# Delta rule inversion: the four steps with 64 wide f32 matmuls, tile by tile, become 128 wide matmuls of two tiles each

## The chip, the cores and the metric

The kernel runs on one core of one Trainium2 chip. The metric is the device time of one execution in microseconds (us), lower is better. A core has a matmul engine (TensorE, PE in the profile, with its weight loads as PEld), a vector engine (DVE), a scalar engine (ACT), GpSimd (POOL) and SyncE (SP, which issues most DMAs). Each engine works through its own queue in order; engines wait for each other by semaphores. Matmuls read their operands from the on-chip memory SBUF and write into PSUM banks, from which ACT and DVE copy results back.

## What is computed

A two-layer decoder trunk over 1024 positions and 1024 channels. The first layer mixes tokens by a gated DeltaNet, the second by a diagonal state-space layer; both run beside a cross-attention into 256 memory tokens, and both are followed by an MLP. The part that matters here is the DeltaNet's delta rule, per head and per chunk:

```
a_strict = jnp.where(strict, jnp.einsum('bhnid,bhnjd->bhnij', kb, k) * decay, 0.0)
sol = lax.linalg.triangular_solve(eye + a_strict, rhs, left_side=True, lower=True, unit_diagonal=True)
u_blk, w_blk = sol[..., :dv], sol[..., dv:]
def step(state, inp):
    v_new = ui - jnp.einsum('bhcd,bhde->bhce', wi, state)
    attn = jnp.einsum('bhid,bhjd->bhij', qi, ki) * deci
    o = (qi * exp(gci)) @ state + attn @ v_new
    state = state * jnp.exp(g_last) + k_dec^T @ v_new
```

There are 8 heads of width 128. The reference takes chunks of 64 positions; the kernel takes tiles of 128 positions, 8 tiles a head, and needs the inverse of one unit triangular 128 x 128 matrix (identity plus strictly triangular part) per head and tile.

## The kernel before

**The work and its stages.** Large products are made with three float32r matmuls each (`mm3`, L362 to L367: high x high, low x high, high x low parts of the operands), 128 x 512 a matmul. Small square products, the inversion among them, are single f32 matmuls. The stages are: projections of the first two heads; attention into the memory; the delta rule (`run`, the loop over heads): while the recurrence of head h runs (`gdn_recur`), the projections of head h + 1, the keys of head h + 3 and the inversion of head h + 1 are woven in as filling (`gdn_fill`); then the output projection, the MLP, and the second layer.

**The inversion.** The 128 x 128 triangular matrix is inverted from small blocks upward. `gdn_inverse` (L1079) inverts the diagonal 32 x 32 blocks of two heads at once on DVE, ACT and POOL and writes them to DRAM (`t32`, once as they are and once transposed), and `gdn_keys_out` (L1037) writes the negated strict part there (`ntf`). `gdn_invert_tiles` (L1169) does the rest, one head at a time in two halves of four tiles. Per half it loads `nm` (parts of `ntf`, three DMAs) and the block diagonals `T32` and `V32` (`block_diag`, L1161, two and four DMAs into the two buffers `bds`, which are cleared once at the start and used again for every half), and makes five steps:

1. `nm` times the first 32 x 32 blocks: four 64 wide matmuls (L1187); the result goes into `zi`, a buffer that begins as the identity, by an ACT copy (L1188) and a DVE copy (L1189).
2. `V32` times `zi`: four 64 wide matmuls (L1195), copied by ACT into the lower half of `o` (L1196).
3. `zi` times `V32`, 128 wide: four matmuls (L1202), copied by ACT into the result `TT` (L1203). It gives both 64 x 64 diagonal blocks of the inverse.
4. `nm`'s off-diagonal 64 x 64 block times `o`: four 64 wide matmuls over 64 rows (L1207), copied by DVE into the upper half of `o` (L1208).
5. `o` times `TT`: four 64 wide matmuls over 64 rows (L1212), copied by ACT into the off-diagonal block of `TT` (L1213).

All matmuls of the inversion are issued by the small helper `mm`, so that the profile has them under its line, L1176, and tells them apart by operands: `iv<-bd,nm`, `iv<-zi,bd`, `iv<-bd,zi`, `iv<-iv,nm`, `iv<-iv,iv`. All five results of a half go through one PSUM bank (tag `pi`, one buffer), so that a step's matmuls wait until the copies of the step before have read it. The buffers `nm`, `o`, `bds` and `zi` are of tag `h4`, which has six.

**What sets the order.** `settle` (L58 on) takes the whole traced program and writes out an order for every engine. It gives each instruction a price (`price`, L276), each PE instruction a due time from its place in the program, every other one a due time counted back from what needs it, and then issues whatever is ready and most pressing, engine by engine; a PE instruction may be taken up to 40 us ahead of its place. Prices of f32 matmuls go by the wider of the two operands, 0.01 us + 1.66 ns a column. A copy out of PSUM is made to wait for a copy by another engine that reads the same bank.

Of the kernel before, what the change touches and what calls it, by code (L numbers as in the profile page):

```python
# [10 lines left out]
F32 = mybir.dt.float32  # L11
# [5 lines left out]
P = 128  # L17
# [13 lines left out]
class Trunk:  # L31
# [810 lines left out]
    def gdn_consts(self):  # L842
        nc = self.nc
        scr = self.tile("scr", [P, 9 * P], F32, "scr")[:, :P + 8 + 13 * 64 + 96]
        self.small = [scr[:, P + 8 + n * 64:P + 8 + (n + 1) * 64] for n in range(13)]
        early = self.tile("h1", [P, 3 * P], F32, "early")
        U = early[:, 0:P]
        nc.gpsimd.memset(U, 1.0)
        nc.gpsimd.affine_select(U, U, [[1, P]], ALU.is_ge, 0.0, base=0, channel_multiplier=-1)
        self.U = U  # L850
        ones = early[:, P:2 * P]
        nc.gpsimd.memset(ones, 1.0)
        self.ones = ones
        mn = scr[:, 0:P]
        nc.gpsimd.memset(mn, 0.0)
        nc.gpsimd.affine_select(mn, mn, [[1, P]], ALU.is_ge, -1e30, base=0, channel_multiplier=-1)
        self.maskneg = mn
        self.early = [early[:, 2 * P + 64 * n:2 * P + 64 * (n + 1)].rearrange("p (t h) -> p t h", t=8) for n in range(2)]
        self.bds = [self.tile("h4", [P, 4, P], F32, "bd") for _ in range(2)]
        for o in self.bds:  # L860
            nc.gpsimd.memset(o, 0.0)
        self.zi = self.tile("h4", [P, 4, P], F32, "zi")
        nc.scalar.copy(self.zi, self.ident.unsqueeze(1).to_broadcast([P, 4, P]))
        cw = scr[:, P + 8 + 13 * 64:].rearrange("p (m j) -> p m j", j=4)
        nc.scalar.dma_start(cw, self.a["cw"])
        self.cw = cw
        ng = self.const("ng", [P, 1])
        nc.scalar.dma_start(ng, self.a["ng"])
        nc.gpsimd.tensor_scalar(ng, ng, 0.5, None, op0=ALU.mult)
        self.ng = ng  # L870
        self.kdd = self.dp.tile([8, 2, P, 4, P], F32, tag="kdd", name="kdd")
        self.ded = self.dp.tile([8, 2, P, 4, P], F32, tag="ded", name="ded")
        self.ntf = self.dp.tile([8, 2, P, 4, P], F32, tag="ntf", name="ntf")
        self.ntd = self.dp.tile([8, 8, 4, 32, 32], F32, tag="ntd", name="ntd")
        self.t32 = self.dp.tile([2, 8, 8, 4, 32, 32], F32, tag="t32", name="t32")
# [285 lines left out]
    def block_diag(self, h, hf, w):  # L1161

        o = self.bds[w]
        for b in (0, 2) if w == 0 else range(4):
            q = slice(32 * b, 32 * b + 32)
            self.nc.sync.dma_start(o[q, :, q], self.t32[w, h, 4 * hf:4 * hf + 4, b].rearrange("t i c -> i t c"))
        return o

    def gdn_invert_tiles(self, h):  # L1169


        nc = self.nc
        first = lambda x: x.rearrange("p (b k c) -> p b k c", b=2, k=2)[:, :, 0, :]
        zi = self.zi
        bank = lambda: self.psum("pi", "iv", (P, 4, P))
        mm = lambda *a: nc.tensor.matmul(*a, start=True, stop=True)  # L1176
        out = self.TT[h] = []
        for hf in range(2):
            nm = self.tile("h4", [P, 4, P], F32, "nm")
            for b in range(2):  # L1180
                nc.sync.dma_start(nm[:, :, 32 * b:32 * b + 32], self.ntf[h, hf, :, :, 64 * b + 32:64 * b + 64])
            nc.sync.dma_start(nm[0:64, :, 64:128], self.ntf[h, hf, 0:64, :, 64:128])
            T32, V32 = self.block_diag(h, hf, 0), self.block_diag(h, hf, 1)

            ps = bank()
            for t in range(4):
                mm(ps[0:64, t, 0:64], nm[:, t, 0:64], first(T32[:, t, :]))  # L1187
            nc.scalar.copy(zi[32:64, :, 0:32], ps[0:32, :, 0:32])  # L1188
            nc.vector.tensor_copy(zi[96:128, :, 64:96], ps[32:64, :, 32:64])  # L1189
            yield 0.5  # L1190

            o = self.tile("h4", [P, 4, 64], F32, "iv")
            ps = bank()
            for t in range(4):
                mm(ps[0:64, t, 0:64], V32[:, t, 0:64], zi[:, t, 0:64])  # L1195
            nc.scalar.copy(o[0:64], ps[0:64, :, 0:64])  # L1196
            yield 0.5

            TT = self.tile("h3", [P, 4, P], F32, "iv")
            ps = bank()  # L1200
            for t in range(4):
                mm(ps[:, t, :], zi[:, t, :], V32[:, t, :])  # L1202
            nc.scalar.copy(TT, ps)  # L1203
            yield 0.8
            ps = bank()
            for t in range(4):
                mm(ps[0:64, t, 0:64], nm[0:64, t, 64:128], o[0:64, t, :])  # L1207
            nc.vector.tensor_copy(o[64:128], ps[0:64, :, 0:64])  # L1208
            yield 0.5
            ps = bank()  # L1210
            for t in range(4):
                mm(ps[0:64, t, 0:64], o[64:128, t, :], TT[64:128, t, 64:128])  # L1212
            nc.scalar.copy(TT[0:64, :, 64:128], ps[0:64, :, 0:64])  # L1213
            out.append(TT)
            yield 0.5

# [1159 lines left out]
```

## Time and profile before

| what | value |
|---|---|
| median of 3 runs | 2592.98 us (2591.11 to 2593.45) |
| the profiled execution | 2591.98 us |
| its span, first to last instruction | 2590.3 us |
| mean granted TensorE clock | 0.995 |
| instructions | 36995 |
| bytes moved by DMA | 425.04 MB |
| PE matmuls at one place, L1176 | 640 records, from 182.4 to 667.2 us |

The profile is of one execution. Its rows give for a group of instructions the line, engine, operation, tiles as out<-in, form, count, then the busy time and the mean of one in ns, and behind the second bar the idle time of the engine just before them, with what ended it. The form of a matmul is first the part of the PE array that it uses, rows * columns, and then the size of what it reads or writes ("128*64 128x64"). A timeline row begins with start and length in us. One f32 matmul stands as two records of PE and two of PEld; a float32r matmul as one. A record's length is longer than the step from one matmul to the next, since they are pipelined.

### The profile page before, as it was taken

How to read it: one execution, taken by the hardware profiler on the slowest of the kernel's cores; microseconds unless marked ns; L12 is line 12 of the kernel's file. 1: busy time of each engine (PE TensorE's matmuls, PEld its weight loads, DVE VectorE, ACT ScalarE, POOL GpSimd, SP SyncE). 2: the span in 40 equal slices, each digit the busy share in tenths (PEclk: the TensorE clock that was granted, in tenths of full speed). 3: DMA queues.
4: the chain of work that ended last, by engine and by line, in shares of the span. 5: the costliest groups of instructions: out<-in, count | busy, mean ns of one | idle time of the engine just before them, and what ended most of it. 6: DMA issues, size and time to landing. Idle time of an engine off the chain costs nothing.

```text
span 2590.3 us, 36995 instructions
## 1 busy us (share of the span) xinstructions
PE 2527.0 (98%) x12525; PEld 2077.9 (80%) x12525; DVE 1968.6 (76%) x3659; ACT 1336.0 (52%) x2969; POOL 327.1 (13%) x445
## 2 busy tenths in 40 slices
PE   8999999999999999999999999989999999999998
PEld 6888788887787778878788888878877888888887
DVE  7675857566789988879988965663888766578779
ACT  6665665665446556454444245562456455454441
POOL 1111111010002123121220112212002000000000
PEclk9999999999999999999999999999999999999999
DMA  5443545455523766477354377764335444574422
GB/s 195 123 134 103 142 128 137 141 172 159 180 82 122 233 207 207 164 259 271 119 171 131 138 243 227 206 210 143 114 106 194 170 156 146 197 268 128 146 87 101
DMA packets 284638, 425.04 MB, mean 164 GB/s; under 512 B 114416, under 2 KB 131008, under 8 KB 284448
## 3 DMA queue, kind: packets, MB, share of 16 engines
q1 hardware_dynamic: 263632, 369.42, 43.5%
q0 software_dynamic: 18048, 48.75, 6.3%
q10 hardware_dynamic: 2768, 4.51, 0.5%
q8 instruction: 98, 1.61, 0.3%
q14 instruction: 92, 0.75, 0.1%
HBM read 286.79 MB, written 135.76 MB: 163 GB/s over the span
## 4 chain that ended last, share of the span: by engine, by line
PE 56%; DVE 5%; issue 2%; DMA 2%; ACT 1%; POOL 1%; SPq 0%; DVEq 0%; POOLq 0%; ACTq 0%
PE q L366 6%; PE q L365 6%; PE q L367 6%; PE pB L365 3%; PE pB L367 3%; PE pB L366 3%; PE pC L367 2%; PE pC L365 2%; PE pC L366 2%; PE pA L367 2%; PE pA L365 2%; PE pA L366 2%; PE wu L366 1%; PE tm L365 1%; PE wu L367 1%
## 5 line engine op out<-in xcount | busy, mean ns | idle before, releaser
L366 PE MATMUL q<-wkl,hkh 128*128 128x512 f32 x784 | 306.5, 391 | 0.9 <-DVE wkl L800 0.9
L365 PE MATMUL q<-wkh,hkh 128*128 128x512 f32 x784 | 306.6, 391 | 0.0
L367 PE MATMUL q<-wkh,hkl 128*128 128x512 f32 x784 | 304.7, 389 | 0.0
L799 ACT CAST wkh<-wr 128x512 fp32r<-128x512 f32 x168 | 104.9, 624 | 239.3 <-PE q L366 194.6
L365 PEld LDWEIGHTS q<-wkh,hkh 128*128 128x128 f32 x784 | 147.1, 188 | 33.5 <-issue 1.9
L366 PEld LDWEIGHTS q<-wkl,hkh 128*128 128x128 f32 x784 | 147.2, 188 | 31.4 <-DVE wkl L800 1.5
L367 PEld LDWEIGHTS q<-wkh,hkl 128*128 128x128 f32 x784 | 147.2, 188 | 30.6 <-issue 0.2
L365 PE MATMUL wi<-xTh,wih 128*128 128x512 f32 x384 | 160.4, 418 | 10.2 <-ACT wih L890 7.2
L800 DVE TENSOR_TENSOR wkl<-wr,wkh 128x512 fp32r<-128x512 f32 x168 | 115.6, 688 | 63.8 <-issue 50.5
L367 PE MATMUL wi<-xTh,wil 128*128 128x512 f32 x384 | 153.6, 400 | 0.5 <-DVE wil L345 0.5
L366 PE MATMUL wi<-xTl,wih 128*128 128x512 f32 x384 | 152.6, 397 | 0.0
L481 POOL TENSOR_TENSOR mv<-mv,mhalf 128x1 f32<-128x1 f32 x32 | 24.6, 767 | 879.0 <-DVE mv L480 879.0
L800 DVE TENSOR_TENSOR hkl<-hr,hkh 128x512 fp32r<-128x512 f32 x196 | 133.9, 683 | 1.9 <-ACT hkh L799 1.9
L799 ACT CAST hkh<-hr 128x512 fp32r<-128x512 f32 x196 | 120.8, 616 | 0.0
L365 PE MATMUL o<-ow,ok 128*128 128x512 f32 x256 | 102.3, 399 | 1.1 <-ACT ok L1608 0.6
L366 PE MATMUL o<-ow,ok 128*128 128x512 f32 x256 | 100.2, 392 | 0.2
L367 PE MATMUL o<-ow,ok 128*128 128x512 f32 x256 | 100.3, 392 | 0.1
L365 PEld LDWEIGHTS wi<-xTh,wih 128*128 128x128 f32 x384 | 72.9, 190 | 23.6 <-ACT wih L890 7.2
L367 PEld LDWEIGHTS wi<-xTh,wil 128*128 128x128 f32 x384 | 72.7, 189 | 15.6 <-DVE wil L345 1.0
L366 PEld LDWEIGHTS wi<-xTl,wih 128*128 128x128 f32 x384 | 73.1, 190 | 11.6
L793 DVE TENSOR_TENSOR y<-q,y 128x512 f32<-128x512 f32 x112 | 72.0, 680 | 0.0
L1608 ACT CAST ok<-os 128x512 fp32r<-128x512 f32 x56 | 34.9, 624 | 54.4 <-PE o L367 41.5
(586 smaller groups left out, 7423.7 us busy)
## 6 DMA issues: line engine op xcount, KB each, us to landing
hr<-hd SPq DMA_DIRECT2D x212, 256.0 KB, 2.6
wr<-in_w_dram SPq DMA_DIRECT2D x56, 512.0 KB, 4.5
w1r<-in_w_dram SPq DMA_DIRECT2D x48, 512.0 KB, 3.8
hd<-u SPq DMA_DIRECT2D x92, 256.0 KB, 2.0
hd<-hid SPq DMA_DIRECT2D x60, 256.0 KB, 3.5
hd<-p SPq DMA_DIRECT2D x60, 256.0 KB, 3.4
w1r<-in_w_dram SPq DMA_DIRECT2D x48, 256.0 KB, 4.7
wir<-in_w_in_dram SPq DMA_DIRECT2D x23, 512.0 KB, 4.0
```

Source lines behind the costliest of these rows:

```text
L365: mm(ps, a[0], b[0], start=start, stop=False, skip_group_check=onto)
L366: mm(ps, a[0], b[1], start=False, stop=False, skip_group_check=onto)
L367: mm(ps, a[1], b[0], start=False, stop=stop, skip_group_check=onto)
L481: nc.gpsimd.tensor_tensor(mv[:, 3:4], mv[:, 2:3], self.mhalf[:, 0:1], op=ALU.pow)
L793: V.tensor_tensor(o, bank[t], o, op=ALU.add)
L799: nc.scalar.copy(hi, s)
L800: nc.vector.tensor_tensor(lo, s, f32(hi), op=ALU.subtract)
L1608: nc.scalar.copy(hi, s)
```

## The change

Tiles are taken in pairs. With `left` of two tiles side by side as the stationary operand (2 x 64 columns) and `right` of the same two tiles as the moving one (2 x 64 columns), one matmul gives a 128 x 128 result, of which the two 64 x 64 corners on the diagonal are the two tiles' products; the other two corners aren't used. So each of steps 1, 2, 4 and 5 has two 128 wide matmuls instead of four 64 wide ones. Step 3 keeps its four.

To make the operands lie side by side, `nm` and `V32` get the layout 2 x 4 tiles x 64 columns. Steps 4 and 5 now go over all 128 rows: `nm[:, 1]` is loaded for all 128 partitions, and the upper half of `o` is cleared by a POOL memset before step 4 so that the added rows give nothing; in step 5 the added rows meet the block of `TT` that is still zero. A pair's two products lie on different partitions of the bank, and so each copy out of it becomes two: even tiles by ACT, odd tiles by DVE in steps 2, 4 and 5, and two by each in step 1.

```diff
-        self.bds = [self.tile("h4", [P, 4, P], F32, "bd") for _ in range(2)]
+        self.bds = [self.tile("h4", shape, F32, "bd") for shape in ([P, 4, P], [P, 2, 4, 64])]
...
-            self.nc.sync.dma_start(o[q, :, q], self.t32[w, h, 4 * hf:4 * hf + 4, b].rearrange("t i c -> i t c"))
+            to = o[q, :, q] if w == 0 else o[q, b // 2, :, 32 * (b % 2):32 * (b % 2) + 32]
+            self.nc.sync.dma_start(to, self.t32[w, h, 4 * hf:4 * hf + 4, b].rearrange("t i c -> i t c"))
...
+        def pairs(left, right):
+            ps = bank()
+            for t in (0, 2):
+                mm(ps[:, t // 2, :], left[:, t:t + 2].rearrange("p t c -> p (t c)"), right[:, t:t + 2])
+            return [ps[64 * x:64 * x + 64, 0:2, 64 * x:64 * x + 64] for x in range(2)]
...
-            nm = self.tile("h4", [P, 4, P], F32, "nm")
+            nm = self.tile("h4", [P, 2, 4, 64], F32, "nm")
             for b in range(2):
-                nc.sync.dma_start(nm[:, :, 32 * b:32 * b + 32], self.ntf[h, hf, :, :, 64 * b + 32:64 * b + 64])
-            nc.sync.dma_start(nm[0:64, :, 64:128], self.ntf[h, hf, 0:64, :, 64:128])
+                nc.sync.dma_start(nm[:, 0, :, 32 * b:32 * b + 32], self.ntf[h, hf, :, :, 64 * b + 32:64 * b + 64])
+            nc.sync.dma_start(nm[:, 1], self.ntf[h, hf, :, :, 64:128])
...
-            ps = bank()
-            for t in range(4):
-                mm(ps[0:64, t, 0:64], nm[:, t, 0:64], first(T32[:, t, :]))
-            nc.scalar.copy(zi[32:64, :, 0:32], ps[0:32, :, 0:32])
-            nc.vector.tensor_copy(zi[96:128, :, 64:96], ps[32:64, :, 32:64])
+            for x, q in enumerate(pairs(nm[:, 0], first(T32))):
+                nc.scalar.copy(zi[32:64, x::2, 0:32], q[0:32, :, 0:32])
+                V.tensor_copy(zi[96:128, x::2, 64:96], q[32:64, :, 32:64])
...
-            ps = bank()
-            for t in range(4):
-                mm(ps[0:64, t, 0:64], V32[:, t, 0:64], zi[:, t, 0:64])
-            nc.scalar.copy(o[0:64], ps[0:64, :, 0:64])
+            nc.gpsimd.memset(o[64:128], 0.0)
+            for x, q in enumerate(pairs(V32[:, 0], zi[:, :, 0:64])):
+                (nc.scalar.copy, V.tensor_copy)[x](o[0:64, x::2], q)
...
-                mm(ps[:, t, :], zi[:, t, :], V32[:, t, :])
+                mm(ps[:, t, :], zi[:, t, :], V32[:, :, t, :])
...
-            ps = bank()
-            for t in range(4):
-                mm(ps[0:64, t, 0:64], nm[0:64, t, 64:128], o[0:64, t, :])
-            nc.vector.tensor_copy(o[64:128], ps[0:64, :, 0:64])
+            for x, q in enumerate(pairs(nm[:, 1], o)):
+                (nc.scalar.copy, V.tensor_copy)[x](o[64:128, x::2], q)
...
-            ps = bank()
-            for t in range(4):
-                mm(ps[0:64, t, 0:64], o[64:128, t, :], TT[64:128, t, 64:128])
-            nc.scalar.copy(TT[0:64, :, 64:128], ps[0:64, :, 0:64])
+            for x, q in enumerate(pairs(o, TT[:, :, 64:128])):
+                (nc.scalar.copy, V.tensor_copy)[x](TT[0:64, x::2, 64:128], q)
```

In the changed file the matmuls' line is L1178, the copies are L1195, L1196 (step 1), L1202 (2), L1209 (3), L1212 (4) and L1215 (5), and the memset is L1200.

More of the change, by code (lines that the diff above doesn't have):

```diff
@@ L1172, in gdn_invert_tiles @@
         nc = self.nc
-        first = lambda x: x.rearrange("p (b k c) -> p b k c", b=2, k=2)[:, :, 0, :]
+        V = nc.vector
+        first = lambda x: x.rearrange("p t (b k c) -> p t b k c", b=2, k=2)[:, :, :, 0, :]
         zi = self.zi
```

## The prediction

> **What bounds the kernel now.** I read the page's busy table first, then the stage in which the inversion runs (180 to 668 us) as one window, then what the matmul engine (PE) waited for in it.
>
> ```profile
> PE 2527.0 (98%) x12525; PEld 2077.9 (80%) x12525; DVE 1968.6 (76%) x3659; ACT 1336.0 (52%) x2969; POOL 327.1 (13%) x445
> ```
> ```profile
> 180.00:668.00 488.00, 479.53 (x2888) 396.05 (x2887) 319.43 (x618) 292.51 (x953) 64.44 (x81) 1.00 0.51 150
> 668.00:2590.30 1922.30, 1879.12 (x8765) 1543.44 (x8763) 1518.59 (x2747) 924.95 (x1694) 237.59 (x317) 1.00 0.51 170
> ```
> ```profile
> PE wi L365 <- ACT qT L1008: 2.8, 2, 1.4
> ...
> PE iv L1176 <- DVE zi L1189: 0.5, 1, 0.5
> ```
>
> The first row is the stage of the inversion, the second the rest; the columns are length, then busy time of PE, its weight loads, DVE, ACT and POOL, then granted clock and DMA share. In the stage PE is busy 479.5 of 488.0 us at clock 1.00; DVE 319, ACT 293, POOL 64. The waits say the same: the longest kind of PE wait is 2.8 us in all, and for the inversion's own copies it waited once, 0.5 us. So here PE's queue sets the time, and what a matmul occupies of it is worth its full length. "Busy" doesn't say how much of that is streaming; for that I measure what a visit of the inversion costs between ordinary matmuls.
>
> **What a narrow visit costs.** I call the matmuls of one step that stand together a visit. It costs the time from the end of the instruction before it to the end of the one behind it, less that one's normal step. Each f32 matmul shows as two records, so x8 is a step of four.
>
> ```profile
> 184.08 0.40 PE L366 MATMUL wi<-xTl,wih 128*128 128x512 f32 x1
> 184.31 0.40 PE L367 MATMUL wi<-xTh,wil 128*128 128x512 f32 x1
> 184.64 0.68 PE L1176 MATMUL iv<-zi,bd 128*64 128x64 f32 x8
> 185.25 0.50 PE L365 MATMUL wi<-xTh,wih 128*128 128x512 f32 x1
> ```
>
> The normal step is 184.71 - 184.48 = 0.23. The visit: L367 ends at 184.71, the next L365 at 185.75; 1.04 - 0.23 = **0.81 us** for four 64 wide matmuls. Where the planner broke a step into one and three, the single one shows alone:
>
> ```profile
> 198.31 0.39 PE L365 MATMUL wz<-xTh,wzh 128*128 128x512 f32 x1
> 198.63 0.33 PE L1176 MATMUL iv<-zi,bd 128*64 128x64 f32 x2
> 198.89 0.50 PE L366 MATMUL wz<-xTl,wzh 128*128 128x512 f32 x1
> ```
>
> From 198.70 to 199.39, 0.69 - 0.23 = 0.46 us for one matmul. Three more cost 0.81 - 0.46 = 0.35, or 0.117 each. So a narrow visit has a **fixed part** of 0.46 - 0.117 = 0.343 us, nearly half of it. Now 128 wide visits, first the inversion's own third step, then four transposes (a record each):
>
> ```profile
> 187.20 0.40 PE L367 MATMUL wi<-xTh,wil 128*128 128x512 f32 x1
> 187.44 1.05 PE L1176 MATMUL iv<-bd,zi 128*128 128x128 f32 x8
> 188.25 0.47 PE L365 MATMUL wi<-xTh,wih 128*128 128x512 f32 x1
> ```
> ```profile
> 652.04 0.40 PE L367 MATMUL wz<-xTh,wzl 128*128 128x512 f32 x1
> 652.27 0.60 PE L1249 MATMUL vt<-ident,vT 128*128 128x128 f32 x4
> 652.63 0.48 PE L365 MATMUL wi<-xTh,wih 128*128 128x512 f32 x1
> ```
>
> The first: 188.72 - 187.60 - 0.23 = 0.89 us for eight records. The second: 653.11 - 652.44 - 0.23 = 0.44 for four. Twice the records cost twice the time: a 128 wide visit has no fixed part, and a 128 wide f32 matmul costs 0.89 / 4 = 0.2225 us. The weight loads' idle time tells the two kinds apart as well (the column behind the bar's second number):
>
> ```profile
> L1176 PEld LDWEIGHTS iv<-bd,zi 128*128 128x128 f32 x128 | 16.5, 191 | 1.3 <-DVE oT L1387 0.3
> ...
> L1176 PEld LDWEIGHTS iv<-zi,bd 128*64 128x64 f32 x128 | 8.9, 137 | 5.3 <-issue 2.2 <-DVE zi L1189 1.6 <-DVE gb L1235 0.4
> L1176 PEld LDWEIGHTS iv<-bd,nm 128*64 128x64 f32 x128 | 8.6, 137 | 5.1 <-issue 2.9 <-DMA bd<-t 0.7 <-ACT iv L1213 0.4
> L1176 PEld LDWEIGHTS iv<-iv,nm 64*64 64x64 f32 x128 | 8.6, 134 | 3.9 <-DVE oT L1387 1.1 <-ACT e L1351 0.7 <-ACT iv L1203 0.4
> L1176 PEld LDWEIGHTS iv<-iv,iv 64*64 64x64 f32 x128 | 8.6, 134 | 4.3 <-issue 2.9 <-DVE S L1360 0.4 <-DVE scr L1229 0.4
> ```
>
> The four narrow groups idle 18.6 us before their loads, the wide one 1.3, with as many records and in the same chain. Only the shape of the array that the matmul asks for differs (128*64 and 64*64 against 128*128). [...]
>
> **The change, part by part.** *Matmuls.* There are 8 heads x 2 halves x 4 narrow steps = 64 steps. In the built order of before they make 68 visits (60 whole, four broken in two): 256 x 0.117 + 68 x 0.343 = 30.0 + 23.3 = 53.3 us. After, all are 128 columns wide, two in a step: 128 x 0.2225 = 28.5. **Saved: 24.8 us**, nearly all of it the fixed part; streaming itself gains 1.5.
>
> *Order.* The planner orders the whole program anew, so other work could move. In the built order of the changed program PE's other matmuls stand as before up to the first inversion and again behind the last one; the same holds for ACT, DVE, POOL and SP. Only the delta rule's stretch is reshuffled. Behind it I count nothing: that stretch starts earlier and takes what it took.
>
> *Copies.*
>
> ```profile
> L1203 ACT COPY iv<-iv 128x512 f32<-128x512 f32 x16 | 9.5, 592 | 12.0 <-PE iv L1176 12.0
> ...
> L1208 DVE COPY iv<-iv 64x256 f32<-64x256 f32 x16 | 6.7, 418 | 12.4 <-PE iv L1176 11.9
> ...
> L1196 ACT COPY iv<-iv 64x256 f32<-64x256 f32 x16 | 5.9, 366 | 15.5 <-PE iv L1176 15.3
> L1213 ACT COPY iv<-iv 64x256 f32<-64x256 f32 x16 | 5.8, 366 | 14.7 <-PE iv L1176 14.4
> L1189 DVE COPY zi<-iv 32x128 f32<-32x128 f32 x16 | 4.6, 287 | 7.0 <-ACT zi L1188 6.8
> L1188 ACT COPY zi<-iv 32x128 f32<-32x128 f32 x16 | 4.1, 255 | 7.0 <-PE iv L1176 6.8
> ```
>
> A step's result now lies in two corners of the bank, so each copy becomes two, split over ACT and DVE. Per half of a head: the copies of 64x256 become ACT 64x128 and DVE 64x128 (128 elements a lane, as L1188 and L1189: 0.255 and 0.287); the first step's two become four of 64 elements a lane, estimated from the slopes between 128 and 256 elements at 0.20 on ACT and 0.22 on DVE. ACT goes from 1.58 to 1.76 us, DVE from 0.71 to 1.30: 2.9 and 9.5 us over 16 halves, beside 195 and 169 us in which they stand idle here. As work that is hidden. As a chain it is longer: L1189 waits for L1188 because both read one bank, so pairs run ACT, then DVE, and the first step ACT, DVE, ACT, DVE. First step 0.54 to 0.84, the next 0.37 to 0.54, the fourth 0.42 to 0.54, the fifth 0.37 to 0.54: 0.76 us a half without the hand-overs, at most **12.2 us** if PE had nothing to do meanwhile, zero if the work that the planner puts between steps covers it. In the new order most steps have 0.9 us or more of other matmuls between them, which covers 0.54 and a hand-over. Two places in head 6 don't: one matmul (0.22) between second and third step, two (0.46) between third and fourth, where the 0.59 copy of L1203 must pass. [...]
>
> *POOL's memset and the wait that it adds.* Sixteen memsets of 64x256; the nearest row is POOL's memset of the 128x512 tiles:
>
> ```profile
> L861 POOL MEMSET bd<- 128x512 f32 x2 | 1.0, 517 | 0.0
> ```
>
> Half the elements, about 0.26 us, 4 us in all on an engine idle 424 here. Each waits until step four of an earlier half has freed its buffer, and holds POOL's queue until then. The tightest place stands ahead of the next pair's "To" memsets:
>
> ```profile
> 252.57 0.99 POOL L1117 MEMSET To<- 128x512 f32 x2
> ```
> ```profile
> 264.48 0.68 PE L1176 MATMUL iv<-iv,nm 64*64 64x64 f32 x8
> ```
> ```profile
> 273.79 0.39 ACT L1123 COPY To<-X 64x64 f32<-64x64 f32 x2
> ```
>
> They would slip from 252.6 to about 265.4 + 0.3 + 1.0 = 266.7; ACT needs them at 273.8, so 7 us remain: zero. Without that cover a late memset would delay the pair's inversion by its lateness.
>
> *DMA.* As many issues as before; one load of each half has 128 partitions instead of 64. It is read in step four only, behind three steps: zero. If it came late, step four would wait for it alone.
>
> **Sum.** 24.8 - 1.5 = 23.3 us. The profiled execution took 2591.98 us (span 2590.3), 1.0 under the median of 2592.98; the difference carries over: 2592.98 - 23.3 = **2569.7 us**.
>
> **Rivals.** *The copies take over*: the longer chain is exposed everywhere. For it: the waits for copies are the one thing that grows, and PE gives up 24.8 us under which they hid. Against it: the 0.5 us above. Fully exposed, 24.8 - 12.2 - 1.5 = 11.1: 2581.9. *The fixed part isn't the shape's*: it belongs to the chain's waits ("issue" stands there as its releaser) and stays. Then 128 x 0.2225 + 66 visits x 0.343 = 51.1 against 53.3, less 1.5 of waits: 0.7 gained, 2592.3. Against it: the third step waits in the same chain without it. [...] *Slower: DVE's queue.* The inversion puts 80 copies on DVE where it had 32, and each stands behind what DVE does at the time, often one of these:
>
> ```profile
> L1010 DVE SCALAR_TENSOR_TENSOR vT<-cv,scr,vT 128x512 f32<-128x512 f32 x48 | 35.9, 747 | 15.6 <-ACT vT L1008 15.4
> ```
>
> If 48 more copies each make PE wait for 0.75 us, that is 36, with the chain 48 us: 2592.98 - 24.8 + 48 = 2616. It decides once more than 24.8 us is exposed, 0.39 per step. Against it: DVE idles a third of this stretch, and the planner knows of the queue.
>
> **How the numbers follow.** Forecast 0.78, copies 0.12, fixed part stays 0.04, DVE's queue 0.04, more gain than summed 0.02. The low end: no added waits and the old 0.5 gone, 25.3; a hundredth of a microsecond in each of 64 visits, 0.6; and the stretch of lowered clock
>
> ```profile
> 560.00:580.00 20.00, 20.00 (x95) 16.72 (x96) 9.99 (x18) 10.06 (x27) 3.75 (x5) 0.91 0.62 155
> ```
>
> gone as well, 20 x 0.09 = 1.8: 27.7, 2565. The high end is the first rival's 2582. A difference of 0.2% is about what a measurement of this kernel can tell from none. Faster by more: forecast, copies and more gain, 0.92; within it 0.04; slower 0.04.
>
> **What would show it.** All inversion matmuls of form 128*128, visits of two at 0.44 to 0.45 us by the same reading, idle time before their loads near that of the third step, the last inversion step, now just ahead of 668 us, some 23 us earlier, and from there to the end the same 1922 us. Wrong: PE waits of many microseconds on L1202, L1212 or L1215, or a 128 wide pair that keeps a 0.3 us gap.

## The result, and the profile after

The changed kernel took 2582.93 us (median of 6, 2580.90 to 2589.03) against 2593.36 us for the kernel before, measured beside it (median of 6, 2591.11 to 2594.96). The ratio is 0.9963 with a 95% interval of 0.9950 to 0.9976: faster by 0.37%, 10.4 us. The forecast was a gain of 23.3 us, so the sign is right and less than half of the gain came; the time lies 0.9 us above the high end of the range. The execution profiled is the slowest of the six, 2589.03 us with a span of 2586.2. Its spans below are to be read with that in mind.

The page of the changed kernel, its busy line, and then two windows, the stage of the inversion and the rest (length, then busy time of PE, its weight loads, DVE, ACT and POOL, granted clock, DMA share, GB/s):

```profile
PE 2516.5 (97%) x12269; PEld 2076.9 (80%) x12269; DVE 1979.2 (77%) x3707; ACT 1340.9 (52%) x3001; POOL 328.3 (13%) x461
```
```profile
180.00:660.50 480.50, 466.36 (x2638) 391.50 (x2638) 331.29 (x670) 298.72 (x990) 71.29 (x98) 0.99 0.54 154
660.50:2586.20 1925.70, 1881.82 (x8765) 1546.50 (x8763) 1518.09 (x2748) 924.92 (x1694) 232.23 (x317) 0.99 0.51 170
```

PE has 256 records less, as 128 f32 matmuls have gone. In the stage it is busy 466.4 us where it was 479.5, but the stage is only 7.5 us shorter: PE now stands idle 14.1 us in it, where it stood idle 8.5. The last inversion step shows the same. The groups of the first and the last step (ns min/median/max, then first and last start in us) say that the forms are the ones announced, all 128*128:

```profile
L1178 PE MATMUL iv<-bd,nm x64: 269/276/377, 183.9 to 639.5; 128*128 128x128 f32 x64
...
L1178 PE MATMUL iv<-iv,iv x64: 270/275/377, 194.4 to 659.8; 128*128 128x128 f32 x64
```

The last step begins at 659.8 us; it was 667.2, so 7.4 earlier and not 23. A visit alone costs what was forecast. In the timeline of PE:

```profile
191.40 1.06 PE L1242 MATMUL qk<-qT,kT 128*128 128x128 f32 x8
192.29 0.61 PE L1178 MATMUL iv<-iv,nm 128*128 128x128 f32 x4
192.66 0.48 PE L365 MATMUL wz<-xTh,wzh 128*128 128x512 f32 x1
```

From 192.46 to 193.14 it is 0.68, less the usual 0.23: 0.45 us for two matmuls, where four narrow ones took 0.81. The idle time before the weight loads (behind the bar, second number) says it for the whole stage. Step 3 stands first:

```profile
L1178 PEld LDWEIGHTS iv<-bd,zi 128*128 128x128 f32 x128 | 16.1, 191 | 2.8 <-DVE iv L1202 1.2 <-DVE oT L1389 0.8
...
L1178 PEld LDWEIGHTS iv<-iv,iv 128*128 128x128 f32 x64 | 9.1, 191 | 1.3 <-DVE iv L1212 0.7
L1178 PEld LDWEIGHTS iv<-bd,nm 128*128 128x128 f32 x64 | 9.0, 190 | 2.3 <-DVE iv L1215 1.3 <-DVE oT L1389 0.3
...
L1178 PEld LDWEIGHTS iv<-iv,nm 128*128 128x128 f32 x64 | 8.5, 191 | 2.4 <-issue 2.3
L1178 PEld LDWEIGHTS iv<-zi,bd 128*128 128x128 f32 x64 | 8.5, 191 | 4.6 <-issue 3.7 <-PE vt L1251 0.8
```

The four steps that were narrow had 18.6 us of it and have 10.6, and what is left has other releasers: the new DVE copies stand among them. What PE waited for in the stage (total us, times, longest) shows where the time came from:

```profile
PE ks L1345 <- DVE S L1362: 4.8, 9, 1.4
PE wi L365 <- ACT qT L1008: 2.8, 2, 1.4
PE kk L1070 <- ACT kd L1060: 1.6, 2, 0.8
PE pe L1351 <- DVE R L1347: 1.0, 1, 1.0
PE iv L1178 <- issue: 1.0, 2, 0.8
PE ks L1345 <- DVE S L1360: 0.8, 2, 0.4
PE iv L1178 <- DVE iv L1202: 0.7, 1, 0.7
```

The longest kind is new: the product of the state with the keys (`ks`) waits for the update of the state on DVE (`S`, L1360 and L1362), 5.6 us in 11 times, where it waited 0.3 us in 2. The inversion's own copies stand there with 0.7.

**Two numbers for each profile.** Recorded idle time is not all that a wait costs (the last section has an example: 0.35 us recorded, 0.61 lost). So I took for every PE row from the first inversion step to the last the time from the end of the row ahead to its own end, and from it the median of that time for the same pair of forms over all 14 profiles. The sum of what exceeds the median is called **waits** below; the stage without them is PE's **own time**.

| kernel | stage, us | own time | waits | of them at `ks` | at the inversion |
|---|---|---|---|---|---|
| before | 485.0 | 471.0 | 14.0 | 1.1 | 0.5 |
| after | 476.2 | 446.9 | 29.3 | 9.2 | 6.9 |

Own time fell by 24.1 us, the 24.8 of the forecast. The waits grew by 15.3 us, where 1.5 had been taken: 8.1 at `ks`, 6.4 at the inversion's own matmuls, 0.8 elsewhere.

A part of what is counted so is not waiting. In the profiles the granted clock falls to half for stretches of mostly 3.4 or 6.8 us (0.50 from 312.60 to 315.90 us of after), and the rows in them exceed their medians. One of the two in the stage of the changed kernel as a window:

```profile
312.00:317.00 5.00, 5.00 (x22) 4.40 (x23) 3.79 (x8) 2.92 (x8) 1.31 (x2) 0.66 0.82 252
```

5 us at a mean of 0.66 lose 1.7 us. By the trace's record of the clock such stretches lose at most 1.7 us in the stage of before, 3.4 in after; none of this lies at `ks` or at the inversion. This profiled execution began the stage 1.5 us later than that of before and took 3.3 us longer behind it (2.9 of them by lowered clock: 12.0 us lost there beside 9.1), so that of the 8.8 us only 4.1 are left in its span (2590.3 to 2586.2). Between the medians the gain is 10.4 us, so at least a part of these 4.8 us belongs to this one execution and not to the change.

### The profile page after: what moved, and what is told of

Its sections match the earlier page's. It is cut to its first block, busy times and chain, and to the rows that moved or that the text cites. A ratio compares the mean times of both kernels' runs of the same rounds, so it can differ in the third digit from the quotient of the medians.

```text
span 2586.2 us, 36642 instructions
## 1 busy us (share of the span) xinstructions
PE 2516.5 (97%) x12269; PEld 2076.9 (80%) x12269; DVE 1979.2 (77%) x3707; ACT 1340.9 (52%) x3001; POOL 328.3 (13%) x461
## 4 chain that ended last, share of the span: by engine, by line
PE 53%; DVE 4%; DMA 2%; ACT 2%; issue 2%; POOL 0%; SPq 0%; DVEq 0%; POOLq 0%; ACTq 0%
PE q L366 7%; PE q L365 7%; PE q L367 7%; PE pB L365 2%; PE pB L366 2%; PE pB L367 2%; PE pC L365 2%; PE pC L366 2%; PE pC L367 2%; PE pA L365 2%; PE pA L366 1%; PE pA L367 1%; PE tm L365 1%; PE tm L366 1%; PE wu L366 1%
## 5 line engine op out<-in xcount | busy, mean ns | idle before, releaser
L366 PEld LDWEIGHTS wi<-xTl,wih 128*128 128x128 f32 x384 | 73.3, 191 | 12.2 <-issue 0.6
```

The costliest lines, as they stand in the source:

```text
L366: mm(ps, a[0], b[1], start=False, stop=False, skip_group_check=onto)
```

## The experiments

The expectations weigh four theories for the 15 us. **A**: the doubled copies, a longer chain on ACT and DVE, are exposed. **B**: the copies don't matter; the order was kept only as long as PE lost 0.34 us in every narrow visit, which the planner had not priced, and now PE keeps to the plan while ACT and DVE come late. **C**: the plan itself is at fault, since it lets PE follow ACT and DVE too closely, by prices that are too low for what reads PSUM. **D**: DVE and ACT bound the stage whatever the order is. Ratios are to the kernel before, run on the same chip in the same group (medians 2595.93, 2594.64 and 2595.09 us in the three groups), each with its 95% interval. Some expectations count the waits in another way, which is not described and comes out some 8 us higher: 22 for before, 38 for after, 30 for wide_old_copies.

**wide_old_copies**: the wide matmuls with the copies as they were, one a step.

```diff
-            return [ps[64 * x:64 * x + 64, 0:2, 64 * x:64 * x + 64] for x in range(2)]
+            return ps[0:64, 0:2, :].rearrange("p t (k c) -> p (t k) c", k=2)
...
-            for x, q in enumerate(pairs(V32[:, 0], zi[:, :, 0:64])):
-                (nc.scalar.copy, V.tensor_copy)[x](o[0:64, x::2], q)
+            nc.scalar.copy(o[0:64], pairs(V32[:, 0], zi[:, :, 0:64]))
...
```

> Paired 128 wide matmuls as in the changed kernel, but one copy per step as before: each copy takes partitions 0 to 63 of both results, so the odd tiles get the unused corners instead of their products (that part of the inversion is changed). Theory A (the added copies lengthen ACT's and DVE's queues and eat the saving): the 15 us of added matmul-engine waits go, about 2569 us. Theory B (ACT and DVE work around the recurrence was just in time already, and whatever makes PE's queue shorter runs into it): the waits stay, 2580 to 2583 us.

Measured: 2578.30 us, ratio 0.9932 (0.9919 to 0.9946). The last step begins at 649.8 us:

```profile
L1178 PE MATMUL iv<-iv,iv x64: 270/275/315, 191.3 to 649.8; 128*128 128x128 f32 x64
```

**narrow_new_copies**: the other half, the 64 wide matmuls of before with two copies a step.

```diff
-            nc.scalar.copy(o[0:64], ps[0:64, :, 0:64])
+            for x, copy in enumerate((nc.scalar.copy, nc.vector.tensor_copy)):
+                copy(o[0:64, x::2], ps[0:64, x::2, 0:64])
...
```

> The 64 wide matmuls of before, each copy split in two over ACT and DVE as in the changed kernel. [...] Theory B: they stay covered, 2592 to 2595 us.

Measured: 2602.83 us, ratio 1.0027 (1.0012 to 1.0043), where theory A had 2596 to 2607. With the two halves by themselves the stage makes a square:

| | one copy a step | two copies a step |
|---|---|---|
| 64 wide | before: 485.0, waits 14.0 | narrow_new_copies: 493.4, waits 22.6 |
| 128 wide | wide_old_copies: 468.7, waits 21.7 | after: 476.2, waits 29.3 |

Two copies instead of one cost some 8 us in either row, but not in the same way. In narrow_new_copies little of it is at `ks` and the inversion (4.2 us together instead of 1.6). `kk`, the product of the keys with themselves, waits for `kd`, which ACT makes, in two places, and behind each the clock is lowered for 6.8 us:

```profile
PE kk L1070 <- ACT kd L1060: 5.2, 2, 2.6
```
```profile
312.00:320.00 8.00, 6.62 (x26) 5.22 (x25) 5.49 (x10) 4.09 (x11) 2.21 (x3) 0.57 0.77 217
```

The wait for `kd` is 1.7 us in before, so that it grew by 3.5; the lowered clock loses at most 6.8 us in this stage instead of 1.7. Together that is as much as the 8.6 us by which the waits grew. Whether the wait brings the lowered clock is not shown.

In the 128 wide row the loss stands where the change works. The waits at `ks` and at the inversion together are 1.6 us in before, about 8 in wide_old_copies (4.6 at `ks`) and 16.1 in after. So neither A nor B explains the 15 us alone; under this plan the wide matmuls by themselves and the doubled copies have about half each.

**full_columns**: four matmuls a step as before, with 64 moving columns, but with 128 stationary ones, so that the array's form is 128*128.

```diff
-                mm(ps[0:64, t, 0:64], V32[:, t, 0:64], zi[:, t, 0:64])
+                mm(ps[:, t, 0:64], V32[:, t, :], zi[:, t, 0:64])
...
```

> Four matmuls per step as before, still 64 columns moving, but with 128 stationary columns and 128 rows, so that all have the form of the whole array; copies as before, one per step; two small memsets on POOL per half. If the fixed part of a narrow visit is the changed shape of the array and a matmul is paid by its moving columns, a visit costs about 0.47 us and the saving is that of the paired matmuls: theory A 2569 us, theory B 2580 to 2583 us. If it is paid by its stationary columns, a visit costs 0.89 and the time is 2595 to 2600 us.

Measured: 2606.18 us, ratio 1.0039 (1.0026 to 1.0053). A visit in PE's timeline:

```profile
189.19 1.06 PE L1242 MATMUL qk<-qT,kT 128*128 128x128 f32 x8
190.08 1.00 PE L1176 MATMUL iv<-iv,nm 128*128 128x64 f32 x8
190.90 0.48 PE L365 MATMUL wz<-xTh,wzh 128*128 128x512 f32 x1
```

From 190.25 to 191.38, less 0.23, it is 0.90 us for four: 0.225 each, the price of a matmul with 128 moving columns (0.2225), not that of a narrow one (0.117). Broken visits of two matmuls cost 0.45 and 0.46 by the same reading, half of 0.90, so there is no fixed part. Two things follow. The fixed part goes with the form alone. And behind 128 stationary columns a f32 matmul costs as much here with 64 moving columns as with 128; I had left the slower of the two answers at 2600, and it came out 6 us above that. 64 visits by 0.09 us are 5.8 of the 10 us, and the stage is 6.4 longer. The granted clock can account for the rest: its median is 0.994 here and 0.996 in the runs of before beside it, which is an estimated 5 us in 2600.

**pair_copies_on_act**: both copies of steps 2, 4 and 5 on ACT, no DVE in the chain.

```diff
-                (nc.scalar.copy, V.tensor_copy)[x](o[0:64, x::2], q)
+                nc.scalar.copy(o[0:64, x::2], q)
...
```

> The changed kernel with both copies of a pair on ACT in steps two, four and five; the first step's stay split. Theory A, if it is DVE's queue that holds back the recurrence's state update: the waits before the ks matmuls shrink, 2574 to 2580 us. If it is ACT's queue: longer waits, 2585 to 2590 us. Theory B: 2580 to 2584 us.

Measured: 2583.13 us, ratio 0.9954 (0.9942 to 0.9967), not to be told from the 0.9963 of the change. The waits are 28.4 (29.3 in after), at `ks` 5.3 instead of 9.2, at the inversion 6.7 instead of 6.9. It eases DVE's queue and gives the time back elsewhere, for instance at `kk`, where the recorded wait for ACT is 3.4 us instead of 1.6; moving the copies to the other engine does not bring the time back.

**after_margin and before_margin**: the planner lets PE work follow what it needs by 0.5 us instead of 0.2, up to the last instruction of the inversion.

```diff
+        stage = max(x for x, i in enumerate(ins) if any(nm.startswith("iv_") for nm in uses(i)))
...
-                    ready[y] = max(ready[y], r + (0.0 if x not in deps[y] else busy if same else length + lag + (margin if ins[y].engine == E.PE else 0.0)))
+                    ready[y] = max(ready[y], r + (0.0 if x not in deps[y] else busy if same else length + lag + ((0.5 if y <= stage else margin) if ins[y].engine == E.PE else 0.0)))
```

> The changed kernel, but the planner counts 0.5 us instead of 0.2 on top of each hand-over to the matmul engine, up to the last inversion step only; behind it the order is that of the changed kernel. [...] Theory D (ACT's and DVE's chains are too long in these places whatever the order): 2580 to 2586 us.

> The kernel before with the same 0.5 us in the plan, up to the last inversion step: the control. It breaks more narrow visits in two (some 20 more, 0.34 us each, 7 us). [...]

Measured: after_margin 2579.28 us, 0.9940 (0.9925 to 0.9956), waits 25.8; before_margin 2599.01 us, 1.0014 (1.0003 to 1.0024), waits 17.5. More reserve helps the changed kernel a little, between the two forecasts (2568 to 2576 us by theory C, 2580 to 2586 by D), and the kernel before not at all (2593 to 2602 by both). The plan has a part in it, but a reserve for everything is not the remedy.

**act_copies_margin**: the two edits together, both copies on ACT and the larger reserve.

> The changed kernel with both copies of a pair on ACT in steps two, four and five, and 0.5 us in the plan for hand-overs up to the last inversion step. If the plan's room and DVE's load add up, this is the fastest of all, 2566 to 2574 us; theory D: 2579 to 2584 us.

Measured: 2582.72 us, 0.9951 (0.9936 to 0.9966), waits 30.0. A miss for the thought that the two would add up.

**after_prices**: the prices themselves. Everything on ACT or DVE that reads PSUM costs the planner 0.1 us more, within the stage (`stage` as above); the kernel's instructions are the same and only their order differs.

```diff
-            cost.append(self.price(i, big))
+            c = self.price(i, big)
+            if x <= stage and i.engine in (E.Activation, E.DVE) and any(self.home.get(q.bass_ap.tensor.name, "s")[0] == "ps" for q in i.ins if getattr(q, "bass_ap", None) is not None):
+                c = c[0] + 0.1, c[1] + 0.1, c[2]
+            cost.append(c)
```

> The changed kernel, but the planner counts 0.1 us more for every copy or operation of ACT and DVE that reads PSUM, up to the last inversion step only. Theory C in the form that these prices are what is wrong: waits in the stage fall from 38 us to 25 to 30, 2570 to 2577 us. Theory D: 2580 to 2586 us.

Measured: **2567.44 us, ratio 0.9898 (0.9880 to 0.9916)**, 27.2 us faster than before, the fastest version of the study and faster than theory C's 2570. The stage as a window, its last step, and its PE waits:

```profile
178.00:643.00 465.00, 456.86 (x2636) 392.34 (x2635) 331.79 (x670) 300.18 (x989) 70.81 (x98) 1.00 0.56 161
```
```profile
L1182 PE MATMUL iv<-iv,iv x64: 270/275/275, 191.4 to 642.3; 128*128 128x128 f32 x64
```
```profile
PE wz L369 <- ACT vT L1012: 2.7, 2, 1.4
PE ks L1349 <- DVE S L1366: 2.3, 1, 2.3
PE iv L1182 <- issue: 1.4, 2, 1.1
PE pe L1355 <- DVE R L1351: 0.4, 2, 0.2
```

DVE and ACT are as busy as in after (331.8 and 300.2 us beside 331.3 and 298.7), with as many copies of the same length. The last step begins 24.9 us earlier than before, and `ks` waits once instead of 11 times. That refutes D: the same work fits under PE in another order.

**before_prices and wide_old_copies_prices**: the same edit of the prices in the kernel before and in wide_old_copies.

> The control to the changed kernel with dearer PSUM reads in the plan: the kernel before with the same 0.1 us more for every ACT and DVE operation that reads PSUM, up to the last inversion step. Narrow visits in its order: 71 instead of 68, 1 us. [...] If the prices are a gain of their own: 2575 to 2585 us.

> Paired matmuls with the copies of before (the odd tiles get the unused corners, that part of the inversion is changed), planned with the dearer PSUM reads. Theory C: the waits fall from 30 to about 22 us, 2567 to 2571 us, and the added copies then cost nothing, since the changed kernel planned so took 2567. If the copies cost by themselves: 2558 to 2563 us.

Measured: before_prices 2596.83 us, 1.0006 (0.9997 to 1.0015), where theory C had 2588 to 2596; wide_old_copies_prices 2568.55 us, 0.9899 (0.9885 to 0.9912).

| stage, waits in us | prices as they are | 0.1 us more |
|---|---|---|
| before | 485.0, 14.0 | 492.5, 19.5 |
| wide_old_copies | 468.7, 21.7 | 466.5, 19.0 |
| after | 476.2, 29.3 | 462.0, 14.2 |

In total the kernel before wins nothing from the prices and both wide kernels do. And with them the doubled copies cost nothing that these runs can tell: 0.9898 and 0.9899.

The totals hide two parts that go against each other. At `ks` and the inversion the dearer prices take the waits from 16.1 us to 6.8 in the changed kernel and from 8.0 to 2.4 in wide_old_copies; the kernel before has 1.6 there, and 3.1 with them. That is where the change lost its time. But the same edit moves ACT's `kd`, and this is the longest wait of before_prices:

```profile
PE kk L1074 <- ACT kd L1064: 8.5, 2, 4.3
```

It is 1.7 us in before, 6.3 in wide_old_copies_prices and absent in after_prices. In before_prices these two places and the lowered clock (at most 8.5 us lost) hold nearly all of the 19.5. So the control shows that the edit gains nothing in all for the kernel before; it doesn't show that its order was left as good everywhere else. And part of the 27.2 us of after_prices is luck: its order has no wait at `kk`.

**after_prices_inversion and after_prices_others**: the 0.1 us for the inversion's copies only, and for all other reads of PSUM only.

```diff
+ ... and q.bass_ap.tensor.name.startswith("iv_")
```
```diff
+ ... and not q.bass_ap.tensor.name.startswith("iv_")
```

> The changed kernel, with 0.1 us more in the plan for the inversion's own copies out of PSUM alone. If the change's added copies are what the plan has too cheap, this gives most of the 27 us, 2567 to 2573 us; if the other PSUM reads are, little, 2578 to 2584 us.

> The changed kernel, with 0.1 us more in the plan for all PSUM reads up to the last inversion step but the inversion's own copies. The mirror of the run before it: 2578 to 2584 us if the added copies are what is too cheap, 2567 to 2573 us if the others are; both near 2575 if each does half.

Measured: 2579.09 us, 0.9934 (0.9922 to 0.9946), waits 25.5; and 2579.83 us, 0.9940 (0.9928 to 0.9953), waits 26.0. Each lies in the range that was expected if the other half is what matters, so the totals name neither: each recovers some 3 to 4 us of waits, both together 15. At `ks` and the inversion, however, each half alone does as much as both: of the 16.1 us there 6.2 are left when the inversion's copies are priced, 3.2 when the others are, 6.8 with both. What they win there they lose elsewhere. after_prices_others waits 6.3 us for `kd`, with the clock lowered for at most 6.8 us lost in its stage; after_prices_inversion waits 3.7 us ahead of `po` for another result of ACT, `on`.

## Why the prediction was right in part and wrong in part

*What bounds the stage* was right: PE's queue. A change of some 23 us in PE's own time shows in full as soon as the waits are no longer than before (after_prices: 485.0 to 462.0 us with waits of 14.2 beside 14.0).

*The price of a narrow visit and the 24.8 us* were right: 24.1 measured. The fixed 0.343 us belongs to the form of the array, as full_columns shows (none of it there in the form 128*128, with 64 moving columns as before), and the rival by which it stays falls. A matmul with 64 moving columns took 0.225 us there behind 128 stationary ones, beside 0.117 behind 64.

*Copies: the sizes* were right. The groups of the changed kernel (busy, mean ns):

```profile
L1196 DVE COPY zi<-iv 32x64 f32<-32x64 f32 x32 | 7.2, 225 | 6.0 <-ACT zi L1195 5.4
...
L1195 ACT COPY zi<-iv 32x64 f32<-32x64 f32 x32 | 6.5, 203 | 12.6 <-PE iv L1178 10.0 <-DVE zi L1196 2.1
...
L1200 POOL MEMSET iv<- 64x256 f32 x15 | 4.6, 307 | 182.4 <-PE iv L1178 147.8 <-DMA bd<-t 34.6
```

The copies of 64 elements take 0.20 and 0.225 us (0.20 and 0.22 estimated), the memset 0.31 (0.26), and no PE wait in the list above names the memset or a load.

***The step that failed is the last of the copies' part: "zero if the work that the planner puts between steps covers it", and the 1.5 us that the sum has for what it doesn't cover.*** The added waits are 15.3 us, 14.5 of them at `ks` and the inversion. The bound of 12.2 beside it was too narrow as well, because it counted only the inversion's own chain. The 1.5 us was an estimate of mine with a hand-over time that no run shows: in the trace of before a copy that waits starts mostly 0.04 us after the recorded end of the visit it waits for, and PE, where it waits for a copy, 0.05 to 0.06 us after the copy's end.

It failed in two ways. First, "for the inversion's own copies it waited once, 0.5 us" came from a run in which PE lost 0.343 us at each of 68 visits, 23 us that the planner does not price. Those 23 us were reserve for ACT and DVE: PE came later than planned, and they had time. By the planner's price four narrow matmuls take 4 x 0.116 = 0.465 us and two wide ones 2 x 0.222 = 0.445, so that in the plan a step hardly changed, while on the chip it went from 0.81 to 0.45. I took the reserve out as gain and kept the 0.5 that it had made possible. wide_old_copies shows this by itself: the waits at `ks` and the inversion rise from 1.6 to about 8 us with no copy added.

Second, "the planner knows of the queue", which I put against the DVE rival, is true of the order and not of the prices. One place shows both. DVE and PE in the changed kernel:

```profile
237.44 0.69 DVE L1071 SCALAR_TENSOR_TENSOR NT<-kk,D 128x512 f32<-128x512 f32 x1 [1.50 <-ACT D L1063]
238.16 0.29 DVE L1215 COPY iv<-iv 64x128 f32<-64x128 f32 x1
238.49 0.35 DVE L1362 SCALAR_TENSOR_TENSOR S<-S,scr,pS 128x128 f32<-128x128 f32 x1
```
```profile
237.33 0.49 PE L1048 MATMUL kt<-ident,kT 128*128 128x128 f32 x3
238.89 0.49 PE L1345 MATMUL ks<-S,kT 128*128 128x128 f32 x2 [1.07 <-DVE S L1362]
```

and the same update and product in the kernel before:

```profile
238.44 0.34 DVE L1360 SCALAR_TENSOR_TENSOR S<-S,scr,pS 128x128 f32<-128x128 f32 x1
```
```profile
239.54 0.39 PE L1343 MATMUL ks<-S,kT 128*128 128x128 f32 x2
```

The state is updated at the same moment, 238.84 and 238.78 us. Before, PE came to `ks` at 239.54 and found it done. Now PE is through with what stands ahead at 237.82 and waits 1.07 us. PE comes 1.7 us earlier, partly because it is faster and partly because the new order has fewer matmuls in front of `ks`. DVE's work ahead, which waits for ACT's `D` in both kernels (1.50 and 1.49 us), begins only 0.39 us earlier, and the inversion's copy in front of the update uses that up. The planner prices that copy on DVE at 0.07 us + 1.04 ns an element (`price`), 0.203 us for 128; from its start to that of the update it is 238.49 - 238.16 = 0.33 us. In narrow_new_copies a copy of the same size stands at the same place, and there the step is 237.56 - 237.35 = 0.21 us:

```profile
237.35 0.28 DVE L1217 COPY iv<-iv 64x128 f32<-64x128 f32 x1
237.56 0.33 DVE L1364 SCALAR_TENSOR_TENSOR S<-S,scr,pS 128x128 f32<-128x128 f32 x1
```

All three such pairs of narrow_new_copies take 0.207 or 0.208 us, all seven of the changed kernel 0.307 to 0.325. In step 5, shown here, both copies write to the same place; what differs is where in the bank they read, partitions 0 to 63 there and 64 to 127 here, since the odd tiles' products now lie in the second corner. So at this place the price fits the copy from partitions 0 to 63 and is 0.1 us short for the one that the change makes. The formula of `price` knows nothing of this, and for DVE it doesn't tell PSUM from SBUF.

That the order is the cause is shown: with the same instructions in another order the waits fall back to 14.2 us. That it is the prices which spoil the order has this for it: dearer PSUM reads take the waits at `ks` and the inversion down in all four wide kernels planned with them. It remains in part argued. One value, 0.1 us for everything, was tried, and the only other change of the plan is the larger reserve of after_margin, which leaves 11.7 of the 16.1 us there. An order reshuffled without any such purpose was not tried, and each half of the edit serves these two places as well as the whole. Apart from DVE's copies above, which prices are off, and by how much, was not separated.

*Order: "Behind it I count nothing"* held as far as the profiled executions tell: from the end of the last inversion step on they took 1922.8 us (before), 1926.1 (after) and 1921.1 (after_prices), of which the lowered clock took at most 9.1, 12.0 and 8.9.

*The rivals.* "The copies take over" gave 2581.9 us, close to the 2582.93 measured, but for another reason than its own, and so by luck: half of the waits come without the added copies, and with dearer prices the longer chain costs nothing that shows. The DVE queue was named with the right engine and the wrong price, 36 us; the wait is at the state's update and not at each copy. *The signs named ahead* were the forms and the visits, which came as written, and the last step 23 us earlier, which did not come and says that something ate the gain. "Many microseconds on L1202, L1212 or L1215" did not come either: the recorded wait stands on the line behind the copy in DVE's queue.

## What to carry to other kernels

Time that an engine loses without the planner's knowledge (here 23 us of PE's) is reserve for all the others; when a change removes it, read the waits of the old trace as if that engine came earlier by as much, and correct the planner's prices in the same step. When a change of the plan is judged by a control, look at where its waits stand and not at the total alone: before_prices gained nothing in all because two waits for `kd` took back what it won. In the changed kernel the correction was worth more than the change showed without it (the ratio went from 0.9963 to 0.9898). In this kernel small f32 matmuls among whole-array ones cost less in the whole array's form, two products in one (0.45 us a visit instead of 0.81), where the two products could be taken from the corners.

## What the runs showed of the hardware that was not expected

- In these traces a f32 matmul with 128 stationary and 64 moving columns costs 0.225 us, as much as one with 128 moving ones (0.2225), while 64 by 64 costs 0.117.
- In these runs a wait costs PE more than the gap that the trace records. Recorded idle time in the stage rose by 5.6 us (8.5 to 14.1), the waits counted from end to end by 15.3, of which the lowered clock can have 1.7. One place in the changed kernel:

```profile
250.70 0.39 PE L367 MATMUL wi<-xTh,wil 128*128 128x512 f32 x1
251.44 0.49 PE L1345 MATMUL ks<-S,kT 128*128 128x128 f32 x2 [0.35 <-DVE S L1362]
```

  From 251.09 to 251.93 it is 0.84 us; without a wait the kernel before takes 0.23 for the same pair (0.39 us from 250.73, ended 251.12, behind an end at 250.89). The wait costs 0.61, and 0.35 are recorded.
- A copy of 128 elements on DVE out of PSUM with the state's update behind it, which reads PSUM too, has a length of 0.28 to 0.29 us. From start to start it takes 0.207 or 0.208 us where it reads partitions 0 to 63 (narrow_new_copies) and 0.307 to 0.325 where it reads 64 to 127 (after), so that only the first overlaps with what follows.
- Stretches at half the granted clock, mostly 3.4 or 6.8 us long, are not the same in each profile: the stage of wide_old_copies has none, that of before_prices loses at most 8.5 us by them. The executions of the kernel before alone have mean granted clocks from 0.992 to 0.998. Differences of a few us between two profiles are to be read with this beside them.
